# Down products of both FFNs in a seven-block form, with sums formed in the gates, in a hybrid decoder block

## The chip, the cores and the metric

The kernel runs on one core of one Trainium2 chip. The metric is the device time of one execution in microseconds (us). Below, TensorE is PE (its weight loads PEld), VectorE is DVE, ScalarE is ACT, GpSimd is POOL, and SyncE is SP, which here only issues DMAs.

## The reference, cut to what matters

One decoder block: a SwiGLU FFN, three mixers in parallel behind one projection, a second SwiGLU FFN, and a final norm. All data is float32; the sequence has 1024 tokens, the model width D is 1024 and the FFN width 2816 (22 tiles of 128).

```python
def _swiglu(h, w_gate, w_up, w_down):
    return (jax.nn.silu(h @ w_gate) * (h @ w_up)) @ w_down

x = x + 0.5 * _swiglu(_rmsnorm(x, ffn1_norm), ffn1_w_gate, ffn1_w_up, ffn1_w_down)
h = _rmsnorm(x, mix_norm)
...                                   # RWKV-7, NSA
y_mem = _memory_branch(q_mem, _rmsnorm(mem, mem_norm), mem_w_k, mem_w_v)   # 256 memory tokens
...                                   # gated merge, x = x + merged @ w_out
x = x + 0.5 * _swiglu(_rmsnorm(x, ffn2_norm), ffn2_w_gate, ffn2_w_up, ffn2_w_down)
return _rmsnorm(x, final_norm)
```

## The kernel before, in words

Everything is held transposed: x is eight strips of 128 features by 1024 tokens, and each strip has two halves of 512 tokens. To keep float32 accuracy on PE every operand is split into a high and a low part (`split`: ACT writes the high part, DVE, or POOL where it is asked to, subtracts it from the source for the low part), and each product of 128 x 128 weights with 128 x 512 data is three matmuls (`mm3`: high x high, high x low, low x high).

An FFN has two stages. The **gates** (class `Gates`) compute silu(gate) * up for the 22 tiles. The first four tiles are computed plainly; the other 18, in nine pairs, by `run`, which already uses a seven-block form: of a 2 x 2 block product it computes seven block products (P1 to P7, of four 128 x 512 products each) in place of eight, from sums and differences of weight blocks that POOL forms (`blocks`, tiles `wS` and `wraw`) and of data blocks that were formed once (`sums`). `finish` makes an activation tile `sg` out of a gate and an up product and SP stores it to HBM (`ad`). One pair of tiles takes two rounds of seven block products, one for gate and one for up; the last two blocks of a round (P4 and P3) are computed in the round behind it.

The **tail** (`Builder.tail`) is the down product. It loads the activations back (`wraw<-ad`), splits them into tiles `a`, loads and splits the down weights (`wd`), and for each strip d of the output and each half accumulates in a PSUM bank `pd` over the tiles of one chunk; DVE then adds a quarter of that to x. The 22 tiles are taken in chunks of 4, 5, 8 and 5. In the last chunk the strips of one half come before those of the other, so that sums of squares, the norm and its splits (`after`, in the background by `tick`) can start early. `xload` reloads x at the tail's start. In the first FFN the tail also normalizes the memory tokens on the side (`aside`, `Mem.tokens`), into tiles `mt` that the memory branch uses right after the tail.

Each engine runs its queue in order; the order in a queue comes out of a scheduler that places the instructions of the program as written. Weight blocks are fetched and split three products ahead (`AHEAD`). The raw weights have eight buffers in the FFN stages, their high and low parts four each. Temporary results of the gates go through a ring of ten buffers (`rg`).

## Time and profile before

| | |
|---|---|
| median of 3 runs | 2943.76 us (2938.05 to 2948.24) |
| profiled execution: its time | 2942.52 us |
| profiled execution: its span | 2940.7 us |
| PE busy | 2836.4 us, 96% of the span |
| DVE, ACT, POOL busy | 60%, 43%, 22% |
| first tail, from first to last `pd` matmul | 471.5 to 713.0 us |
| second tail | 2682.2 to 2923.9 us |

The profiled execution's own time is 1.8 us above its span. Busy shares are means over stages; which engine is waited for has to be read from each stage. A matmul's own duration overlaps that of the next, so the time that one costs is read from the number of matmuls in a stretch.

### The profile page before, as it was taken

Reading aid. Unit: us, or ns where it says so; the run is one execution under the profiler, and the core shown is the slowest. Engines: PE = TensorE matmul, PEld = TensorE weight load, DVE = VectorE, ACT = ScalarE, POOL = GpSimd, SP = SyncE. Lnnn points to the kernel's source line nnn. Section 1 sums busy time; section 2 is a strip of 40 time slices with the busy share of each in tenths; the row PEclk is TensorE's granted clock in tenths of the full one; section 3 lists DMA queues with packets and bytes.
Section 4 is the critical chain, followed back from the end, with each engine's and each line's share of the span. In section 5 each row is a group of like instructions: output and inputs, shape, how many; then the busy total and the mean of one; then the engine's idle time right before and its main releaser. Section 6 shows DMA issues by size and latency. Waiting matters only on the chain. (4 is left out here: it accounts for less than half of the span.)

```text
span 2940.7 us, 39952 instructions
## 1 busy us (share of the span) xinstructions
PE 2836.4 (96%) x13790; PEld 2252.7 (77%) x13790; DVE 1755.4 (60%) x3794; ACT 1276.1 (43%) x2743; POOL 638.0 (22%) x717
## 2 busy tenths in 40 slices
PE   7899999999999999999999989999998999999997
PEld 5788888887887777767767667778777888888886
DVE  8555555627566656766555357888857555555526
ACT  5333333315454445544443356666544333333313
POOL 3422220004011011111110133433323422220002
PEclk9999999999999999999999998999999999999999
DMA  4222226515313222222221552221475222225413
GB/s 154 76 85 84 86 78 203 162 36 150 96 61 91 60 66 71 65 73 63 65 65 59 158 169 77 84 60 58 145 224 177 90 86 79 83 83 193 141 41 106
DMA packets 203047, 294.41 MB, mean 100 GB/s; under 512 B 46131, under 2 KB 75707, under 8 KB 202844
## 3 DMA queue, kind: packets, MB, share of 16 engines
q1 hardware_dynamic: 186384, 263.25, 29.1%
q10 hardware_dynamic: 16460, 28.61, 3.3%
q8 instruction: 108, 1.77, 0.3%
q14 instruction: 95, 0.78, 0.1%
HBM read 223.51 MB, written 68.27 MB: 99 GB/s over the span
## 5 line engine op out<-in xcount | busy, mean ns | idle before, releaser
L99 ACT ACTIVATE whi<-wraw 128x512 fp32r<-128x512 f32 x576 | 345.3, 603 | 755.0 <-PE pgu L120 283.1
L102 DVE TENSOR_TENSOR wlo<-wraw,whi 128x512 fp32r<-128x512 f32 (+1 forms) x568 | 411.8, 729 | 375.2 <-ACT whi L99 349.5
L119 PE MATMUL mm<-h,whi 128*128 128x512 f32 x800 | 330.1, 413 | 0.2 <-ACT gbt L1553 0.2
L121 PE MATMUL mm<-h,wlo 128*128 128x512 f32 x800 | 320.6, 402 | 7.2 <-DVE wlo L102 7.2
L120 PE MATMUL mm<-h,whi 128*128 128x512 f32 x800 | 318.7, 398 | 0.0
L119 PE MATMUL pgu<-h,whi 128*128 128x512 f32 x688 | 272.5, 396 | 19.5 <-ACT whi L99 18.6
L121 PE MATMUL pgu<-h,wlo 128*128 128x512 f32 x688 | 271.9, 396 | 9.2 <-DVE wlo L102 9.1
L121 PE MATMUL pd<-a,wlo 128*128 128x512 f32 x704 | 274.2, 390 | 1.7 <-DVE wlo L102 1.7
L120 PE MATMUL pgu<-h,whi 128*128 128x512 f32 x688 | 272.0, 396 | 2.2 <-DVE h L94 1.7
L120 PE MATMUL pd<-a,whi 128*128 128x512 f32 x704 | 273.9, 389 | 0.0
L119 PE MATMUL pd<-a,whi 128*128 128x512 f32 x704 | 273.9, 389 | 0.0
L119 PE MATMUL pgu<-t,whi 128*128 128x512 f32 x576 | 224.3, 389 | 2.1 <-ACT rg L412 2.1
L120 PE MATMUL pgu<-t,whi 128*128 128x512 f32 x576 | 224.1, 389 | 0.0
L121 PE MATMUL pgu<-t,wlo 128*128 128x512 f32 x576 | 224.1, 389 | 0.0
L132 POOL TENSOR_TENSOR acc<-acc,sq 128x512 f32<-128x512 f32 x46 | 68.1, 1481 | 578.6 <-ACT sq L131 575.5
L121 PEld LDWEIGHTS mm<-h,wlo 128*128 128x128 f32 x800 | 151.6, 190 | 39.9 <-DVE wlo L102 9.0
L119 PEld LDWEIGHTS mm<-h,whi 128*128 128x128 f32 x800 | 151.8, 190 | 36.4 <-issue 5.3
L120 PEld LDWEIGHTS mm<-h,whi 128*128 128x128 f32 x800 | 151.9, 190 | 28.6 <-issue 3.0
L119 PEld LDWEIGHTS pgu<-h,whi 128*128 128x128 f32 x688 | 131.5, 191 | 49.4 <-ACT whi L99 21.6
L256 DVE SCALAR_TENSOR_TENSOR x<-pd,x 128x512 f32<-128x512 f32 x128 | 87.7, 688 | 130.2 <-PE pd L121 126.3
L121 PEld LDWEIGHTS pgu<-h,wlo 128*128 128x128 f32 x688 | 131.1, 191 | 40.3 <-DVE wlo L102 13.0
L121 PEld LDWEIGHTS pd<-a,wlo 128*128 128x128 f32 x704 | 132.2, 188 | 30.4 <-DVE wlo L102 3.0
(401 smaller groups left out, 6071.5 us busy)
## 6 DMA issues: line engine op xcount, KB each, us to landing
wraw<-in_wgu SPq DMA_DIRECT2D x192, 256.0 KB, 2.6
wraw<-in_wd SPq DMA_DIRECT2D x96, 256.0 KB, 2.7
ad<-sg SPq DMA_DIRECT2D x88, 256.0 KB, 2.8
wraw<-ad SPq DMA_DIRECT2D x88, 256.0 KB, 2.7
wraw<-in_win SPq DMA_DIRECT2D x52, 256.0 KB, 2.6
wraw<-in_wgb SPq DMA_DIRECT2D x48, 256.0 KB, 2.8
gd<-gbt SPq DMA_DIRECT2D x48, 256.0 KB, 2.0
gbt<-gd ACTq DMA_DIRECT2D x40, 256.0 KB, 2.7
```

The source lines that it names most:

```text
L99: nc.scalar.activation(hi, src, AF.Copy)
L102: (nc.vector if eng_lo == "dve" else nc.gpsimd).tensor_sub(lo, src, hi.bitcast(FT))
L119: mm(ps, w[0], x[0], start=start, stop=False, **kw)
L120: mm(ps, w[0], x[1], start=False, stop=False, **kw)
L121: mm(ps, w[1], x[0], start=False, stop=stop, **kw)
L132: eng.tensor_add(acc, acc, sq)
L256: nc.vector.scalar_tensor_tensor(x[d][:, c], p, 0.25, x[d][:, c], op0=OP.mult, op1=OP.add)
```

## The change

The down product of the tiles 4 to 21 takes the seven-block form too: output strips are taken in pairs (2dp, 2dp+1), tiles in pairs, tokens in halves. Seven block products over a chunk of three pairs of tiles (nine matmuls each) take the place of eight. The data blocks that this needs (the tile itself for three of the blocks, differences of the pair's four tiles for the other four) are formed in the gates by POOL, four subtractions for each pair, and stored: seven tiles for each pair where there were four. The weight sums of a chunk are formed in the tail by POOL, on 128 x 384 tiles. Of the seven products three go to x through ACT (a copy scaled by a quarter) and POOL (an addition), the other four as before through DVE. The first four tiles stay plain and come last. In the tail PSUM has seven banks where there were four; activations are kept in eight groups of three tiles, with four raw buffers (`ar`), and every second tile of three gets its low part from POOL. `sg` has seven buffers where it had five. The memory tokens are normalized in the first FFN's gates, stored to HBM (`td`), and fetched after the tail.

```diff
-CHUNKS = (("a", 4), ("p", 5), ("h", 8), ("p", 5))
+ORDER = "P1", "P2", "P6", "P5", "P7", "P3", "P4"
+NG = 8
+SG = 7
...
+        slots = [(self.hp, f"h{p}0{k}") for k in range(KT) for p in range(2)]
+        slots += [(ap, f"a{n}") for n in range(6 * NG - 32)]
+        slots += [(self.hp, f"h{p}1{k}") for k in range(KT) for p in range(2)]
+        bank = lambda: pool.tile([128, HALF], FT, name="pd", tag="dn", bufs=7)
+        temp = lambda tag, n, bufs: ap.tile([128, n], FT, name=tag, tag=tag, bufs=bufs)
+        groups = [ad[2 + 3 * c + j, name] for c in range(3) for name in ORDER for j in range(3)]
+        groups += [ad[f, half] for half in range(2) for f in range(4)]
+        def load(g):
+            for j, src in enumerate(groups[3 * g:3 * g + 3]):
...
+                if g < 3:
+                    raw = self.wraw(src, HALF)
+                else:
+                    raw = temp("ar", HALF, 4)
+                    nc.sync.dma_start(raw, src)
+                self.split(*t, raw, eng_lo="pool" if j == 1 else "dve")
+        def blocks(c, dp):
+            a = {(i, q): self.wraw(wd[2 * dp + i, :, (6 * c + 3 * q) * 128:(6 * c + 3 * q + 3) * 128], 384)
+                 for i, q in ((0, 0), (0, 1), (1, 0), (1, 1))}
+            yield self.wparts(a[0, 0])
+            yield self.wparts(a[0, 1])
+            s1, s2 = temp("ds", 384, 4), temp("ds", 384, 4)
+            nc.gpsimd.tensor_add(s1, a[1, 0], a[1, 1])
+            nc.gpsimd.tensor_sub(s2, s1, a[0, 0])
+            yield self.wparts(s2)
+            yield self.wparts(s1)
+            nc.gpsimd.tensor_sub(a[1, 0], a[0, 0], a[1, 0])
+            yield self.wparts(a[1, 0])
+            nc.gpsimd.tensor_sub(a[0, 1], a[0, 1], s2)
+            yield self.wparts(a[0, 1])
+            yield self.wparts(a[1, 1])
+        def copy_add(d, half, ps):
+            t = temp("dc", HALF, 4)
+            nc.scalar.activation(t, ps, AF.Copy, scale=0.25)
+            xd = x[d][:, halves[half]]
+            nc.gpsimd.tensor_add(xd, xd, t)
+        ops = [(c, dp, g, c * 7 + g) for c in range(3) for two in range(2) for g in range(7) for dp in (2 * two, 2 * two + 1)]
...
+        for g in range(3):
+            load(g)
+        for dp in range(2):
+            for d in (2 * dp, 2 * dp + 1):
+                xload(d)
+        for g in range(3, NG):
+            load(g)
+        for n, (c, dp, i, g) in enumerate(ops):
+            while len(got) < min(len(ops), n + 1 + AHEAD):
+                pull()
...
+            for k in range(3):
+                self.mm3(ps, [a[:, k * 128:k * 128 + 128] for a in w], act[3 * g + k], ...)
...                                       # P1, P6, P7: copy_add; P2, P5, P3, P4: add
+            if dp == 3 and 3 * (g + NG) < len(groups):
+                load(g + NG)
+        for half in range(2):
+            for d in range(KT):
+                w = self.wload(wd[d, :, 18 * 128:22 * 128], 512)
+                ps = bank()
+                for f in range(4):
+                    self.mm3(ps, [a[:, f * 128:f * 128 + 128] for a in w], act[63 + 4 * half + f], f == 0, f == 3)
+                add(d, half, ps)
+                self.tick()
+                after(half, d)
... Gates.finish
-        nc.sync.dma_start(self.ad[f][half], sg)
+        pair, n = f // 2, f % 2 * 2 + half
+        q = self.act.setdefault(pair, {})
+        q[n] = sg
+        if n != 1:
+            nc.sync.dma_start(self.ad[pair, ("P1", None, "P2", "P3")[n]], sg)
+        if len(q) == 4:
+            a11, a12, a21, a22 = [q[j] for j in range(4)]
+            t = {j: self.ring() for j in ("P5", "P7", "P6", "P4")}
+            nc.gpsimd.tensor_sub(t["P5"], a12, a11)
+            nc.gpsimd.tensor_sub(t["P7"], a22, a12)
+            nc.gpsimd.tensor_sub(t["P6"], a22, t["P5"])
+            nc.gpsimd.tensor_sub(t["P4"], a21, t["P6"])
+            for j in t:
+                nc.sync.dma_start(self.ad[pair, j], t[j])
... Gates.run
+            if i > 20 and i % 5 == 0:
+                next(aside, None)
... Mem.tokens
-                B.split(self.hi[k + e], self.lo[k + e], a)
+            t = [ring().bitcast(FR) for _ in range(2)]
+            B.split(*t, raw)
+            for p in range(2):
+                nc.sync.dma_start(self.td[p][k:k + 2].rearrange("e p n -> p e n"), ...)
+    def fetch(self, tp):
+        self.hi, self.lo = [[tp.tile([128, 256], FR, name=f"mt{p}{k}") for k in range(KT)] for p in range(2)]
+        for k in range(KT):
+            for p, t in enumerate((self.hi, self.lo)):
+                self.nc.sync.dma_start(t[k].bitcast(FT), self.td[p][k])
```

Three places in the queues show what this does to the order.

**SP where the first FFN's gates end and its tail begins, before.** `ad<-sg` stores an activation tile, `x<-in_xT` reloads a strip of x, `wraw<-ad` loads an activation tile, `wraw<-in_wd1` down weights.

```order
L106 DMA wraw_4086<-ad70_165 128x512 [waits DMAHW5_49,DMAHW4_49,DVE_49]
L324 DMA ad211_194<-sg_3663 128x512 [waits DVE_49]
L324 DMA ad210_193<-sg_3707 128x512 [waits DMAHW6_49,DVE_49]
L106 DMA wraw_4090<-ad71_166 128x512 [waits DMAHW7_49,DMAHW1_49,DVE_49]
L324 DMA ad201_192<-sg_3749 128x512 [waits DMAHW0_49,DVE_49]
L106 DMA wraw_4047<-in_wd1 128x512 [waits DVE_49]
L106 DMA wraw_4094<-in_wd1 128x512 [waits DMAHW2_49,DVE_49]
L1530 DMA x0_3843<-in_xT 128x1024 [waits DMAHW3_49,PE_49]
L1530 DMA x1_3844<-in_xT 128x1024 [waits DMAHW4_49]
```

The same place now (`rg_4025` to `rg_4028` are the four differences of the last pair, `ar<-ad2P5` and the two behind it the three tiles of the fourth group, P5):

```order
L381 DMA ad10P2_216<-sg_3900 128x512 [waits DMAHW4_49,DVE_49]
L390 DMA ad10P5_218<-rg_4025 128x512 [waits DMAHW5_49,Pool_49]
L390 DMA ad10P7_219<-rg_4026 128x512 [waits DMAHW6_49,Pool_49]
L390 DMA ad10P6_217<-rg_4027 128x512 [waits DMAHW7_49,Pool_49]
L390 DMA ad10P4_221<-rg_4028 128x512 [waits DMAHW0_49,Pool_49]
L1610 DMA x0_4044<-in_xT 128x1024 [waits DMAHW1_49,PE_49]
L1610 DMA x1_4045<-in_xT 128x1024 [waits DMAHW2_49]
L1610 DMA x2_4046<-in_xT 128x1024 [waits DMAHW3_49]
L1610 DMA x3_4047<-in_xT 128x1024 [waits DMAHW4_49]
L248 DMA ar_4118<-ad2P5_162 128x512 [waits DMAHW5_49,DVE_49]
L248 DMA ar_4124<-ad3P5_169 128x512 [waits DMAHW6_49]
L248 DMA ar_4130<-ad4P5_176 128x512 [waits DMAHW7_49]
```

The reloads of x and the loads of the fourth group now stand behind four stores that wait for POOL, where the x reloads stood behind a store that waits for DVE.

**POOL at the same place, before.** The last weight sums of the gates, then the first work of the tail's end (sums of squares, `acc`):

```order
L375 TENSOR_TENSOR wS_3686<-wS_3685,wraw_3599 128x512 [waits DMAHW1_49,DVE_49,Pool_49]
L378 TENSOR_TENSOR wraw_3603<-wraw_3599,wraw_3603 128x512
L381 TENSOR_TENSOR wraw_3601<-wraw_3601,wS_3686 128x512 [waits DMAHW3_49,DVE_49,Pool_49]
L132 TENSOR_TENSOR acc_4321<-acc_4321,sq_4383 128x512 [waits Activation_49]
L132 TENSOR_TENSOR acc_4321<-acc_4321,sq_4446 128x512 [waits Activation_49,Pool_49]
```

And now (the four differences of the last pair, the four weight sums of the first pair of strips, `ds` and `wraw`, additions to x, the low part of a P5 tile):

```order
L385 TENSOR_TENSOR rg_4025<-sg_3942,sg_3759 128x512 [waits DVE_49,Pool_49]
L386 TENSOR_TENSOR rg_4026<-sg_3856,sg_3942 128x512 [waits DMAHW4_49]
L387 TENSOR_TENSOR rg_4027<-sg_3856,rg_4025 128x512 [waits Pool_49]
L388 TENSOR_TENSOR rg_4028<-sg_3900,rg_4027 128x512 [waits Pool_49]
L259 TENSOR_TENSOR ds_4251<-wraw_4210,wraw_4212 128x384 [waits DMAHW7_49,DMAHW5_49,PE_49]
L260 TENSOR_TENSOR ds_4252<-ds_4251,wraw_4206 128x384 [waits DMAHW1_49,PE_49,Pool_49]
L263 TENSOR_TENSOR wraw_4210<-wraw_4206,wraw_4210 128x384
L265 TENSOR_TENSOR wraw_4208<-wraw_4208,ds_4252 128x384 [waits DMAHW0_49,DMAHW4_49,Activation_49,Pool_49]
L277 TENSOR_TENSOR x0_4044<-x0_4044,dc_4248 128x512 [waits DMAHW1_49,Activation_49]
L277 TENSOR_TENSOR x0_4044<-x0_4044,dc_4321 128x512 [waits Activation_49]
L277 TENSOR_TENSOR x2_4046<-x2_4046,dc_4269 128x512 [waits DMAHW3_49]
L104 TENSOR_TENSOR act311_4123<-ar_4124,act310_4122 128x512 [waits DMAHW6_49,DMAHW2_49,Activation_49]
```

POOL had nothing to do at the tail's start and now has a row of work in which additions wait for x to land and a split waits for a P5 tile. The four weight sums of the second pair of strips stand right behind the last row.

**POOL in the middle of the first gates, before:** the weight sums of two rounds.

```order
L374 TENSOR_TENSOR wS_3385<-wraw_3303,wraw_3305 128x512 [waits DMAHW3_49,DMAHW2_49]
L375 TENSOR_TENSOR wS_3386<-wS_3385,wraw_3299 128x512 [waits DMAHW5_49,DVE_49,Pool_49]
L378 TENSOR_TENSOR wraw_3303<-wraw_3299,wraw_3303 128x512
L374 TENSOR_TENSOR wS_3535<-wraw_3455,wraw_3457 128x512 [waits DMAHW7_49,DMAHW6_49,DVE_49]
L378 TENSOR_TENSOR wraw_3455<-wraw_3451,wraw_3455 128x512 [waits DMAHW1_49,DVE_49,Pool_49]
L381 TENSOR_TENSOR wraw_3301<-wraw_3301,wS_3386 128x512 [waits DVE_49]
```

And now:

```order
L441 TENSOR_TENSOR wS_3567<-wraw_3485,wraw_3487 128x512 [waits DMAHW5_49,DMAHW4_49]
L442 TENSOR_TENSOR wS_3568<-wS_3567,wraw_3481 128x512 [waits DMAHW7_49,DVE_49,Pool_49]
L445 TENSOR_TENSOR wraw_3485<-wraw_3481,wraw_3485 128x512
L385 TENSOR_TENSOR rg_3469<-sg_3320,sg_3137 128x512 [waits DVE_49]
L386 TENSOR_TENSOR rg_3470<-sg_3234,sg_3320 128x512 [waits DMAHW3_49]
L387 TENSOR_TENSOR rg_3471<-sg_3234,rg_3469 128x512 [waits Pool_49]
L388 TENSOR_TENSOR rg_3472<-sg_3278,rg_3471 128x512 [waits Pool_49]
L441 TENSOR_TENSOR wS_3717<-wraw_3637,wraw_3639 128x512 [waits DMAHW1_49,DMAHW0_49,Activation_49]
L445 TENSOR_TENSOR wraw_3637<-wraw_3633,wraw_3637 128x512 [waits DMAHW3_49,Activation_49,Pool_49]
L448 TENSOR_TENSOR wraw_3483<-wraw_3483,wS_3568 128x512 [waits DVE_49]
```

The four differences of the pair before stand between the third weight sum of one round and the first of the next; the fourth sum of the first round (`wraw_3483<-wraw_3483,wS_3568`) stands three rows behind them.

## Rows read from the trace of the kernel before

**Rows 1.** The page's first part: busy time, share of the span and instructions of each engine.

```profile
PE 2836.4 (96%) x13790; PEld 2252.7 (77%) x13790; DVE 1755.4 (60%) x3794; ACT 1276.1 (43%) x2743; POOL 638.0 (22%) x717
```

**Rows 2.** Busy time by stretches (start and end, length, then for each engine busy time and number of instructions, the granted clock, the DMA share, GB/s): three stretches of the first tail, and the second FFN's gates.

```profile
471.00:500.00 29.00, 29.00 (x130) 24.02 (x129) 17.53 (x28) 8.28 (x14) 0.00 (x0) 1.00 0.84 298
...
550.00:600.00 50.00, 50.00 (x222) 41.43 (x221) 28.29 (x54) 16.59 (x32) 0.00 (x0) 1.00 0.47 147
600.00:650.00 50.00, 50.00 (x223) 41.40 (x222) 12.29 (x19) 5.83 (x10) 0.00 (x0) 1.00 0.12 33
...
2440.00:2682.00 242.00, 240.97 (x1064) 199.27 (x1062) 129.17 (x185) 94.44 (x163) 60.40 (x45) 1.00 0.31 95
```

**Rows 3.** The instructions that touch `pd`, by stretches of the two tails (columns PE, PEld, DVE, clock, DMA share, GB/s).

```profile
471.00:715.00 244.00, 240.52 (x1056) 198.04 (x1056) 43.14 (x63) 1.00 0.42 131
2682.00:2930.00 248.00, 240.03 (x1056) 198.18 (x1056) 43.87 (x64) 0.99 0.36 112
```

**Rows 4.** Who waited for whom from 470 to 700 us (us in total, times, longest us); PE is in none of the rows.

```profile
ACT whi L99 <- PE pd L120: 89.3, 32, 7.8
...
ACT a L99 <- DMA wraw<-ad: 32.6, 14, 10.3
```

**Rows 5.** Groups of instructions by form (out<-in, count, then busy us and mean ns of one), from the answers for POOL and ACT over the whole span and for DVE from 471 us on.

```profile
L374 POOL TENSOR_TENSOR wS<-wraw 128x512 f32<-128x512 f32 x36 | 46.5, 1291 | 207.6 <-DMA wraw<-in_wgu 175.1 <-DVE wlo L102 32.5
...
L788 POOL TENSOR_TENSOR bk<-k,ecs 128x128 f32<-128x128 f32 x32 | 14.3, 447 | 17.0 <-PE sm L792 10.1 <-DVE k L724 6.8
...
L99 ACT ACTIVATE whi<-wraw 128x512 fp32r<-128x512 f32 x528 | 331.4, 630 | 740.0 <-PE pgu L120 283.1 <-PE pd L120 195.8 <-PE mm L120 106.9
...
L99 ACT ACTIVATE whi<-wraw 128x128 fp32r<-128x128 f32 x48 | 14.7, 307 | 15.0 <-PE pd L120 13.6
...
L102 DVE TENSOR_TENSOR a<-wraw,a 128x512 fp32r<-128x512 f32 x80 | 52.7, 689 | 27.9 <-ACT a L99 27.7
```

**Rows 6.** The timeline around 61 us, where DVE and POOL both have work (start us, duration us, instruction, count); `sg<-sg,pgu` reads PSUM, the other DVE rows read two SBUF tiles.

```profile
61.25 1.67 POOL L349 TENSOR_TENSOR x<-rg,x 128x512 f32<-128x512 f32 x1 [3.64 <-DVE h L102]
...
67.98 3.41 POOL L349 TENSOR_TENSOR x<-rg,x 128x512 f32<-128x512 f32 x2
71.35 3.38 POOL L350 TENSOR_TENSOR rg<-rg 128x512 f32<-128x512 f32 x2
...
59.89 0.68 DVE L102 TENSOR_TENSOR wlo<-wraw,whi 128x512 fp32r<-128x512 f32 x1
60.49 1.28 DVE L102 TENSOR_TENSOR h<-x,h 128x512 fp32r<-128x512 f32 x2
...
63.40 3.47 DVE L102 TENSOR_TENSOR h<-x,h 128x512 fp32r<-128x512 f32 x2
66.79 0.68 DVE L321 TENSOR_TENSOR sg<-sg,pgu 128x512 f32<-128x512 f32 x1
...
70.19 3.42 DVE L102 TENSOR_TENSOR h<-x,h 128x512 fp32r<-128x512 f32 x2
```

**Rows 7.** The timeline where the first gates end and the tail begins: PE's first `pd` matmul, DVE's last sum and product of the gates and its first addition to x, SP's issues (duration is that of all in the row), and ACT's first activation split that waited.

```profile
471.52 0.39 PE L119 MATMUL pd<-a,whi 128*128 128x512 f32 x1
...
471.72 0.69 DVE L416 TENSOR_TENSOR rg<-pgu,rg 128x512 f32<-128x512 f32 x1 [1.43 <-PE pgu L121]
472.44 0.69 DVE L321 TENSOR_TENSOR sg<-sg,rg 128x512 f32<-128x512 f32 x1
...
481.10 2.63 DVE L256 SCALAR_TENSOR_TENSOR x<-pd,x 128x512 f32<-128x512 f32 x4 [1.94 <-DMA x<-in_xT]
...
474.80 3.71 SPq L1530 DMA_DIRECT2D x<-in_xT  x6
478.92 0.92 SPq L106 DMA_DIRECT2D wraw<-ad  x2
...
488.09 1.27 ACT L99 ACTIVATE a<-wraw 128x512 fp32r<-128x512 f32 x2 [10.25 <-DMA wraw<-ad]
```

**Rows 8.** DMA issues (count, KB each, median us from issue to landing).

```profile
wraw<-ad SPq DMA_DIRECT2D x88, 256.0 KB, 2.7
...
x<-in_xT SPq DMA_DIRECT2D x8, 512.0 KB, 7.9
```

**Rows 9.** The first gates: a row of the waits from 100 to 470 us, and two of POOL's timeline (in brackets its idle time before, and what ended it).

```profile
ACT whi L99 <- PE pgu L120: 159.5, 90, 4.1
...
395.38 1.74 POOL L378 TENSOR_TENSOR wraw<-wraw 128x512 f32<-128x512 f32 x1
404.30 1.29 POOL L374 TENSOR_TENSOR wS<-wraw 128x512 f32<-128x512 f32 x1 [7.19 <-DMA wraw<-in_wgu]
```

**Rows 10.** Busy time by short stretches behind the first tail (columns as in rows 2).

```profile
718.00:720.00 2.00, 0.53 (x5) 0.33 (x3) 1.97 (x2) 1.10 (x3) 0.81 (x1) 1.00 0.76 208
720.00:723.00 3.00, 1.90 (x7) 1.33 (x8) 2.89 (x6) 2.51 (x7) 1.73 (x2) 0.88 0.49 130
723.00:726.00 3.00, 3.00 (x16) 2.90 (x16) 0.81 (x2) 0.96 (x3) 3.00 (x3) 0.55 0.49 114
```

**Rows 11.** PE's first matmuls behind the first tail: the memory branch's keys, and a wait of the projections among them.

```profile
712.81 0.28 PE L119 MATMUL S<-mt,whi 128*128 128x256 f32 x1
...
720.40 0.40 PE L962 MATMUL mm<-wvh,h 128*128 128x280 f32 x1 [1.87 <-ACT wvh L99]
```

More of the change, by code (lines that the diff above doesn't have):

```diff
@@ L224, in tail @@
         ap = st.enter_context(self.tc.tile_pool(name="ffa", bufs=1, reuse_waits="tile"))
-        ps = st.enter_context(self.tc.tile_pool(name="ffd", bufs=1, space=PSUM, reuse_waits="tile"))
-        def parts(kind, j):
-            if kind == "p":
-                return [[ap.tile([128, HALF], FR, name=f"a{p}{j}{half}") for p in range(2)] for half in range(2)]
-            a, b = divmod(j, 4)
-            return [[self.hp.tile([128, HALF], FR, name=f"a{p}{j}{half}", tag=f"h{p}{a}{2 * b + half}")
-                     for p in range(2)] for half in range(2)]
@@ L258, in tail @@
[L258 to L285 removed]
+        pool = st.enter_context(self.tc.tile_pool(name="ffd", bufs=1, space=PSUM, reuse_waits="tile"))
@@ L1473, in body @@
     nc.vector.tensor_copy(B.ones, one)
-    M = Mem(B, A, lambda m, j: yd[2][m][j // 2][:, (j % 2) * 256:(j % 2) * 256 + 256])
+    td = [drp.tile([KT, 128, 256], FT, name=f"td{p}") for p in range(2)]
+    M = Mem(B, A, lambda m, j: yd[2][m][j // 2][:, (j % 2) * 256:(j % 2) * 256 + 256], td)
     def ring_of(st):
@@ L1532, in body @@
                           lambda half, d: nc.sync.dma_start(x1d[d][:, halves[half]], x[d][:, halves[half]])),
[L1533 removed]
+                   st)
     with ExitStack() as mid:
@@ L1565, in body @@
         with ExitStack() as st:
+            mt = st.enter_context(tc.tile_pool(name="met", bufs=1, reuse_waits="tile"))
+            M.fetch(mt)
             M.open(st)
```

123 lines of the change are left out of this document (59 added, 64 removed).

## The prediction

> **What bounds the kernel now.** I read the page's busy shares first: PE is busy 96% of the span, the others 60% and less [rows 1]. Then the stretches, since only a stage tells what work taken from PE is worth there. In both tails PE is busy in every microsecond at full clock, one matmul for each 0.225 us (222 in 50 us), and ACT, DVE and POOL have room [rows 2, 3]. Then the waits of the first tail: ACT waits for PE to free weight buffers, 89.3 us in all, and for activation loads; PE waits for nobody [rows 4]. The gates look alike: 241 of 242 us busy [rows 2], ACT waiting for PE [rows 9]. So these stages end with PE, and a matmul less is worth its 0.225 us as long as what the change hands to POOL, DVE, ACT and the queues stays ahead of PE. The sum below is made against the profiled execution, 2942.5 us, which is 1.2 us under the median of 2943.8.
>
> **What it removes.** Of the tail's 1056 matmuls [rows 3], 18 tiles x 8 strips x 2 halves x 3 = 864 become seven eighths, 756: 108 fewer in each tail, 216 in all. At 0.225 us that is **-48.6 us**. Everything else gives some of it back.
>
> **The start of each tail: +13 us each.** Let 0 be the tail's first matmul (471.5 in the first tail). The last activation of the gates is done at +1.6 (472.44 + 0.69) [rows 7]. Now POOL forms four differences. One such subtraction takes 1.29 us alone [rows 5] and 1.70 where DVE works beside it (two in 3.41) [rows 6]; four take 5.2 to 6.8, and I take 6.2 since DVE has some splits there: +7.8. Until then SP's queue is blocked by the fourth store, and behind it stand four reloads of x and the three tiles of the fourth group (P5). Issues follow each other by 0.62 us (six in 3.71) [rows 7], so they go out from +8.4 to +12.1. They are 2.75 MB, and the queue moved 298 GB/s at this place before [rows 2], so 9.2 us: the P5 tiles have landed at about +17.6. The rows have the same pile-up: two activation loads issued at 478.92 behind 3 MB of x were waited for until 488.09, 9.2 us [rows 7]. It cost nothing then, as four tiles fed PE for 192 matmuls, 43 us; now three groups feed it for six products of nine matmuls, 12 us.
>
> PE meanwhile: four products to +8.1. The fifth (P6 of the first pair of strips) needs two weight sums that stand behind the differences on POOL. A 128x384 sum is no row; between 447 ns (128 columns) and 1291 (512) [rows 5] the line gives 1.01 us. So +9.8, with ACT's split (0.52, on the line from 307 to 630) +10.3: PE idles 2.2 us and ends this product at +12.4. P5 starts after a split of 0.63 [rows 5] at +18.2, 5.8 us idle. Then the second pair of strips: its sums stand on POOL behind additions that wait for x and behind the low part of the second P5 tile (ACT at +18.9, POOL +20.2); two sums make it +22.2, three ACT splits +23.8, and 18 matmuls, P5 and P6 mixed, end at +27.8. Eight products unhindered take 16.2: 11.6 us late. An idle PE also loses its clock: behind the first tail, after 1.5 us idle of 2, 0.88 and then 0.55 was granted in the next two stretches of 3 us, most of the second at the lower of its two levels, 1.2 GHz [rows 10]: 1.7 us lost; here a part falls into waiting, so 1.3. Bounds: 7.8, if the P5 tiles land 2.7 us after their issue like a median load [rows 8] (2.8 less), POOL runs undisturbed (1 less) and the clock stays; 16.9, if two more strips of x (1 MB, 3.4 us) get ahead of them and POOL is always disturbed.
>
> **The middle of each tail: +3 us each.** DVE and POOL disturb each other where DVE reads two SBUF tiles: at 61 to 75 us both backlogged, each does one instruction per 1.70 us, where DVE alone needs 0.60 (59.89 to 60.49), so one of POOL keeps DVE out for 1.10; a DVE row with a PSUM input in between took its usual 0.68 [rows 6]. On 384 columns I scale to 0.83 and 0.45. In the second half of a chunk (14 products, 28.4 us of PE) POOL has 8 weight sums, 6 additions and 7 splits, 20.9 us, DVE 14 weight and 14 activation splits, 14.7: 35.6 us that can't lie beside each other, 7.2 too many. The first half has 19.5. Only the first two chunks have such a full half; the third loads 8 tiles in place of 21. Weights are ready three products ahead, 6.1 us, and the POOL results of that half are needed later, so most is made up in the half behind: I take 1.5 us for each full half. Bounds: 0 and 7.2.
>
> **The smaller terms: +3.5 us together.** In the second half of the first tail's end DVE has per output tile a weight split, an addition, a normalization and its split, 4 x 0.60 = 2.4, and POOL's sum of squares, 1.10, against 12 matmuls, 2.7: 0 to 0.8 for 8 tiles, 1.5 in all. Before, 15 matmuls (3.4) covered it. The fetch of the memory tokens: half of its 16 loads stand on SP behind the last store of x, so they land up to 8 x 0.62 + 2.7 = 7.7 us after the tail. The keys followed the tail at once [rows 11], but projections of the first half can go between, and waits of 1.9 us stood there already: 1, bounds 0 and 5. The gates: POOL's chain ends at most 1.6 + 6.8 = 8.4 us after a pair's last product; the first sum behind it that PE needs is three POOL instructions on, about +13, and its product starts six products of 12 matmuls later, at +16.2. POOL idled for stretches of 7 us [rows 9]. The extra stores and the memory tokens' instructions also lie beside PE. I take 1 for all this. Edits at nothing: `sg` buffers, the weights' new order in HBM, three PSUM banks more; they add no instruction, and work that PE is busy with covers any wait of theirs.
>
> Sum: 2942.5 - 48.6 + 26 + 6 + 3.5 = 2929.4, **2929 us**.
>
> **Rivals.** *The loads are hidden after all (2908 us).* The start then costs only the 2.2 us before the fifth product, 10.8 less in each tail. For it: SP's queue is shared, but 16 engines may serve small loads before the strips of x. Against it: the activation loads of before, which waited as long as the bytes ahead of them.
>
> *DVE and POOL decide the middle (2952 us, slower).* If the 7.2 us of a full half reach PE wholly, a tail loses 14.4 in place of 3: +22.8. It decides from the point where DVE's low parts of the weights are more than three products (6.1 us) late. For it: DVE's queue has activation splits between the weight splits, and when POOL has a backlog each DVE split pays 1.10 first. Against it: most POOL results are needed half a chunk later, and the first half of a chunk has 8.9 us to spare. The Trainium skill's page "SBUF — State Buffer", section "SBUF: two separate sides", states this rule: the port pair that DVE and GpSimd share is an exclusive lock held for a whole instruction, also against a DVE instruction with two SBUF inputs. By that rule with nothing made up the time would be this 2952; the trace agrees with the lock (1.70 against 0.60), and how much of it reaches PE no row shows.
>
> *The chains in the gates reach PE (2976 us, slower).* If half of 5.2 us of differences stood before a needed sum in each of 18 pairs, that is 47 us. It decides where the needed sum is later than +16.2. For it: POOL waits on loads, which an SP queue with three more stores per pair delays. Against it: 3 us of margin by the order, and 60 of 242 us that POOL is busy [rows 2].
>
> **How the numbers follow.** Forecast 0.50, with a range of its own of 2918 to 2942; hidden loads 0.20; DVE and POOL 0.20; gates 0.10. A measurement here can tell about 0.3%, 8.8 us. Below 2935 lie 0.37 of the forecast and all of the hidden loads: faster 0.57. Within lie 0.13 of the forecast, 0.08 of the DVE and POOL case and 0.02 of the gates: same 0.23. Slower 0.20. The range, 2904 to 2953, leaves out the best third of the hidden loads (0.06), the worse third of DVE and POOL (0.06) and most of the gates (0.08).
>
> **What would show it.** 948 `pd` matmuls in each tail. In the first 30 us of each tail two idle stretches of PE, about 2 and 6 us, the longer ended by ACT's split of an activation tile that waited for its DMA, and x reloads issued about 8 us after the first `pd` matmul. DVE splits above 1 us in the second half of the first two chunks. No new wait of PE in the gates. I am wrong if the x reloads go out earlier, if PE waits for low parts of weights all through the chunks, or if the gates become longer.

## The result, and the profile after

The changed kernel takes 2958.1 us (median of 10 runs, 2954.1 to 2965.4) against 2941.9 us of the kernel before beside it (2938.1 to 2950.0): 1.0055 of its time, 95% interval 1.0042 to 1.0069. It is slower, where 2929 us and a gain were forecast. The profiled execution took 2956.2 us with a span of 2954.4, 13.7 above the span before.

The busy times of the page of the changed kernel, beside [rows 1]:

```profile
PE 2804.6 (95%) x13574; PEld 2212.6 (75%) x13574; DVE 1943.0 (66%) x3852; ACT 1369.7 (46%) x2923; POOL 1041.9 (35%) x1005
```

PE has its 216 matmuls fewer and is 32 us less busy, yet the span grew: PE now waits, which it did not do in the tails before. Where, the first tail by stretches shows (the view of [rows 2]: start and end, length, then busy time and instructions of PE, PEld, DVE, ACT and POOL, granted clock, DMA share, GB/s):

```profile
485.00:500.00 15.00, 8.57 (x20) 5.67 (x20) 9.42 (x10) 5.69 (x11) 10.39 (x9) 0.59 0.72 260
...
530.00:560.00 30.00, 24.70 (x101) 17.75 (x99) 28.51 (x30) 16.52 (x32) 24.65 (x18) 1.00 0.63 192
...
590.00:620.00 30.00, 29.08 (x129) 23.57 (x127) 29.98 (x31) 18.40 (x36) 22.84 (x16) 1.00 0.61 186
...
650.00:680.00 30.00, 30.00 (x134) 24.82 (x134) 20.07 (x26) 13.19 (x25) 11.31 (x8) 1.00 0.37 104
```

An undisturbed stretch of 30 us holds 134 matmuls (last row). From 485 to 500 us only 20 run, in place of 67, at a granted clock of 0.59; from 530 to 560, where DVE is busy 28.5 of 30 us and POOL 24.7, 101 run. From 590 to 620 DVE and POOL are about as busy, and 129 run.

For comparing kernels I use two stretches of the first tail and count `pd` matmuls: the first 58 us from its first matmul ("start") and the next 120 ("middle"; nothing is lost later). The columns are PE and PEld, DVE, ACT where it has rows, clock, DMA share, GB/s. The kernel before, then the changed one:

```profile
471.50:529.50 58.00, 57.98 (x256) 48.05 (x256) 13.20 (x20) 1.00 0.65 217
529.50:649.50 120.00, 119.69 (x529) 98.89 (x529) 18.33 (x27) 1.00 0.32 95
```

```profile
472.50:530.50 58.00, 46.69 (x176) 35.77 (x177) 5.45 (x8) 4.66 (x8) 0.85 0.63 213
530.50:650.50 120.00, 111.45 (x474) 87.32 (x473) 21.85 (x32) 13.34 (x23) 1.00 0.49 147
```

The start is 80 matmuls short, 18.0 us at 0.225 us each, and the middle 55, 12.4 us. The forecast had 13 and 3. These counts differ from run to run: in e1_spread, e8_fetch_act and e15_after_banks (the three repeats, below), whose queues have the changed kernel's order in the tail, the start is 72, 67 and 70 short and the middle 62, 53 and 57. The rest of the change is small: the first tail begins 1.0 us later (472.5, before 471.5), the part between the tails is 1.0 us longer, the part behind the second 2.1.

**The start.** PE's long waits, what SP, POOL, ACT and DVE did (start us, duration, in brackets the idle time before and what ended it):

```profile
474.65 1.29 POOL L385 TENSOR_TENSOR rg<-sg 128x512 f32<-128x512 f32 x1 [14.04 <-DVE sg L371]
...
475.97 4.18 SPq L390 DMA_DIRECT2D ad10P<-rg  x4
480.24 1.82 SPq L1610 DMA_DIRECT2D x<-in_xT  x4
482.16 0.39 SPq L248 DMA_DIRECT2D ar<-ad2P  x1
...
482.13 0.63 ACT L101 ACTIVATE act<-wraw 128x512 fp32r<-128x512 f32 x1 [9.09 <-DMA ad10P<-rg]
...
483.71 0.80 PE L121 MATMUL pd<-act,whi 128*128 128x512 f32 x1 [2.85 <-ACT whi L101]
490.47 0.80 PE L121 MATMUL pd<-act,whi 128*128 128x512 f32 x1 [1.20 <-ACT act L101]
494.30 0.79 PE L122 MATMUL pd<-act,whi 128*128 128x512 f32 x1 [3.03 <-DVE act L104]
501.23 0.80 PE L123 MATMUL pd<-act,wlo 128*128 128x512 f32 x1 [2.50 <-DVE wlo L104]
...
492.51 0.69 DVE L271 SCALAR_TENSOR_TENSOR x<-pd,x 128x512 f32<-128x512 f32 x1 [5.58 <-POOL x L277]
```

The chain is the one forecast: POOL's differences, SP's four stores, then the reloads of x (7.7 us behind the first matmul, forecast 8.4) and P5's loads; the fifth product begins at +11.2 us (forecast 10.3) and P5 at +17.9 (18.2). Two things were not in it. ACT's split of the ninth activation tile waited for the fourth store, since the tile lies in the memory that this store reads. And the low parts of P5 stood in DVE's queue behind an addition that waited for POOL's addition to the same strip. Nor was the clock's share as small as I took it. PE's granted clock in stretches of 2 us (PE, clock, DMA share, GB/s):

```profile
482.00:484.00 2.00, 0.29 (x1) 0.93 0.91 330
484.00:486.00 2.00, 1.02 (x3) 0.50 1.03 416
486.00:488.00 2.00, 2.00 (x5) 0.50 1.02 405
488.00:490.00 2.00, 1.27 (x3) 0.50 1.05 403
490.00:492.00 2.00, 0.80 (x1) 0.50 0.82 327
492.00:494.00 2.00, 0.00 (x0) 0.50 0.00 0
494.00:496.00 2.00, 1.70 (x4) 0.50 0.24 48
496.00:498.00 2.00, 2.00 (x7) 0.65 0.80 282
498.00:500.00 2.00, 0.72 (x4) 1.00 0.97 274
500.00:502.00 2.00, 0.77 (x2) 0.70 0.67 199
502.00:504.00 2.00, 2.00 (x7) 0.50 0.44 125
```

After 2.85 us without work it stood at 0.50, the lower of its two levels (1.2 GHz), from 484 to 496, although PE worked for all of 486 to 488, and again from 502 to 504, behind the idle 2.5 us before 501.2. By the spacing of the `pd` matmuls in these 58 us, 23 of them came 0.3 to 0.6 us after the one before, most of these 0.43, which I count as 5.0 us lost to the clock, and six gaps above 0.7 us lost 13.1; in the second tail 24 and five, 4.7 and 11.2.

**The middle.** Who waited for whom, PE in the 120 us of the middle (us in total, times, longest), and POOL and DVE between 543 and 549 us:

```profile
PE pd L123 <- DVE wlo L104: 7.9, 11, 2.1
PE pd L121 <- ACT whi L101: 0.5, 1, 0.5
```

```profile
543.31 0.54 DVE L104 TENSOR_TENSOR wlo<-wraw,whi 128x384 fp32r<-128x384 f32 x1
...
547.63 1.36 DVE L104 TENSOR_TENSOR wlo<-wraw,whi 128x384 fp32r<-128x384 f32 x1
...
544.58 1.01 POOL L259 TENSOR_TENSOR ds<-wraw 128x384 f32<-128x384 f32 x1 [2.34 <-DVE act L104]
...
547.12 1.45 POOL L260 TENSOR_TENSOR ds<-ds,wraw 128x384 f32<-128x384 f32 x1
```

At 543.31 POOL has nothing to do and DVE's low part takes 0.54 us; at 547.63 POOL works and the same instruction takes 1.36. In the first tail as a whole (groups by form: count, busy us, mean ns):

```profile
L104 DVE TENSOR_TENSOR act<-ar,act 128x512 fp32r<-128x512 f32 x41 | 53.6, 1311 | 3.0 <-ACT act L101 2.9
L104 DVE TENSOR_TENSOR wlo<-wraw,whi 128x384 fp32r<-128x384 f32 x57 | 53.2, 940 | 9.0 <-ACT whi L101 9.0
L271 DVE SCALAR_TENSOR_TENSOR x<-pd,x 128x512 f32<-128x512 f32 x62 | 42.5, 685 | 31.0 <-PE pd L123 21.7 <-POOL x L277 9.1
L104 DVE TENSOR_TENSOR wlo<-ds,whi 128x384 fp32r<-128x384 f32 x24 | 27.3, 1145 | 3.4 <-ACT whi L101 3.4
```

An activation split took 0.69 us before [rows 5] and takes 1.31. PE waits for low parts of weights.

Where in the chunks it waits, the starts of the `pd` matmuls show. A half of a chunk is 14 products, 126 matmuls, which took 28.6 us in the kernel before. What each half took beyond that:

| half | first tail, us | second tail, us |
|---|---|---|
| first of chunk 1 (the start) | 17.9 | 15.3 |
| second of chunk 1, full | 6.2 | 6.4 |
| first of chunk 2 | 3.5 | 4.2 |
| second of chunk 2, full | 0.0 | 0.2 |
| first of chunk 3 | 3.5 | 3.5 |
| second of chunk 3 | 0.0 | 0.0 |

PE's waits in the first halves of chunks 2 and 3 (553.8 to 585.8 and 614.4 to 646.4 us), the same row twice, and one of DVE's rows in the second of these:

```profile
PE pd L123 <- DVE wlo L104: 2.2, 4, 0.9
```

```profile
623.53 1.16 DVE L104 TENSOR_TENSOR act<-ar,act 128x512 fp32r<-128x512 f32 x1 [0.26 <-ACT act L101]
```

So only the first of the two full halves loses time itself. The second loses nothing, but DVE still makes its activation splits 9 us into the half behind it (623.5, that half begins at 614.4), and PE meets late low parts in the first five products there. Behind the first full half it is the same.

### The profile page after: what moved, and what is told of

It reads as the page before. It is cut to its first block, busy times and chain, and to the rows that moved or that the text cites. A ratio compares the mean times of both kernels' runs of the same rounds, so it can differ in the third digit from the quotient of the medians.

```text
span 2954.4 us, 40599 instructions
## 1 busy us (share of the span) xinstructions
PE 2804.6 (95%) x13574; PEld 2212.6 (75%) x13574; DVE 1943.0 (66%) x3852; ACT 1369.7 (46%) x2923; POOL 1041.9 (35%) x1005
## 5 line engine op out<-in xcount | busy, mean ns | idle before, releaser
L104 DVE TENSOR_TENSOR wlo<-wraw,whi 128x512 fp32r<-128x512 f32 (+1 forms) x576 | 463.0, 807 | 294.8 <-ACT whi L101 281.0
L101 ACT ACTIVATE whi<-wraw 128x512 fp32r<-128x512 f32 (+1 forms) x584 | 352.9, 607 | 650.1 <-PE pgu L122 252.7
L123 PE MATMUL pd<-act,wlo 128*128 128x512 f32 x632 | 253.6, 402 | 23.5 <-DVE wlo L104 23.1
L121 PE MATMUL pd<-act,whi 128*128 128x512 f32 x632 | 250.2, 396 | 10.5 <-ACT whi L101 6.8
L122 PE MATMUL pd<-act,whi 128*128 128x512 f32 x632 | 249.6, 395 | 5.2 <-DVE act L104 5.2
L122 PEld LDWEIGHTS mm<-h,whi 128*128 128x128 f32 x800 | 151.4, 189 | 28.5 <-issue 3.0
L123 PEld LDWEIGHTS pd<-act,wlo 128*128 128x128 f32 x632 | 121.0, 191 | 63.8 <-DVE wlo L104 38.8
L121 PEld LDWEIGHTS pgu<-h,whi 128*128 128x128 f32 x688 | 131.6, 191 | 49.2 <-ACT whi L101 21.6
L122 PEld LDWEIGHTS pgu<-h,whi 128*128 128x128 f32 x688 | 131.1, 191 | 31.9 <-DVE h L96 2.7
L121 PEld LDWEIGHTS pd<-act,whi 128*128 128x128 f32 x632 | 120.6, 191 | 37.5 <-ACT whi L101 9.4
```

Of the source, the lines that this page charges most:

```text
L101: nc.scalar.activation(hi, src, AF.Copy)
L104: (nc.vector if eng_lo == "dve" else nc.gpsimd).tensor_sub(lo, src, hi.bitcast(FT))
L121: mm(ps, w[0], x[0], start=start, stop=False, **kw)
L122: mm(ps, w[0], x[1], start=False, stop=False, **kw)
L123: mm(ps, w[1], x[0], start=False, stop=stop, **kw)
```

## The experiments

"Short" is the count of `pd` matmuls under 256 in the start and under 529 in the middle of the first tail.

| run | time, us | of the kernel before, 95% interval | short: start, middle |
|---|---|---|---|
| changed kernel | 2958.1 | 1.0055 (1.0042 to 1.0069) | 80, 55 |
| e1_spread | 2958.0 | 1.0052 (1.0030 to 1.0075) | 72, 62 |
| e2_act_stores | 2961.2 | 1.0070 (1.0045 to 1.0095) | 81, 57 |
| e3_no_sums | 2936.0 | 0.9986 (0.9974 to 0.9998) | 81, 2 |
| e4_add_dve | 2940.6 | 0.9998 (0.9985 to 1.0010) | 58, 28 |
| e5_tokens_only | 2954.7 | 1.0040 (1.0021 to 1.0059) | 0, -2 |
| e6_diff_dve | 2951.6 | 1.0034 (1.0021 to 1.0048) | 60, 46 |
| e7_start | 2973.5 | 1.0111 (1.0087 to 1.0134) | 80, 58 |
| e8_fetch_act | 2958.8 | 1.0060 (1.0043 to 1.0077) | 67, 53 |
| **e9_adds_diff** | **2930.2** | **0.9962 (0.9949 to 0.9975)** | 55, 22 |
| e10_adds_diff_p5 | 2934.0 | 0.9977 (0.9967 to 0.9986) | 60, 16 |
| e11_adds_diff_met | 2932.1 | 0.9967 (0.9955 to 0.9979) | 47, 26 |
| e12_all | 2928.9 | 0.9968 (0.9951 to 0.9984) | 58, 12 |
| e13_banks | 2931.8 | 0.9965 (0.9952 to 0.9978) | 53, 25 |
| e14_banks_met | 2933.0 | 0.9965 (0.9953 to 0.9978) | 43, 32 |
| e15_after_banks | 2960.2 | 1.0049 (1.0033 to 1.0066) | 70, 57 |

### The middle: POOL's work taken away, or moved

e3_no_sums, which leaves out the sums of down weights (cut):

```
-  nc.gpsimd.tensor_add(s1, a[1, 0], a[1, 1])     # and the three
-  nc.gpsimd.tensor_sub(s2, s1, a[0, 0])          # others like it
-  yield self.wparts(s2); yield self.wparts(s1)
+  yield self.wparts(a[1, 0]); yield self.wparts(a[1, 1])
```

> The changed kernel without the four sums and differences of down weights on POOL: the products P6, P5, P7 and P3 take plain blocks of the weights, so the output is not the reference's. DVE, ACT and PE have the same instructions as before, POOL 24 per half chunk pair fewer (8 in each half of a chunk). Theory (POOL keeps DVE out, and only therefore are the low parts late): splits of 384 columns on DVE fall from a mean of 0.81 us to about 0.65, the later loss of each tail falls from 14 or 15 us to 3 to 6, the start loses 2 to 3 us less because no sum stands behind the differences, and the time is 2928 to 2938. Rival (DVE has too much work of its own in these halves): the later loss stays above 10 us and the time is 2945 to 2957.

Its middle, columns as above:

```profile
529.30:649.30 120.00, 119.91 (x527) 98.50 (x526) 22.50 (x33) 15.09 (x26) 1.00 0.48 144
```

The middle holds 527 matmuls with all of DVE's instructions in place: its loss is gone, and 22 us of the time. (By halves from the second on it loses 1.9, 0.0, 0.0 and 0.8 us.) The start, 81 short, did not gain. This alone does not part POOL's hold on DVE from the time that PE waits for a sum as such. In e4_add_dve the sums stay, DVE gets more work, POOL less.

```
-  copy_add(2 * dp, 0, ps)         # P1; P6 and P7 likewise
+  add(2 * dp, 0, ps)
```

> The changed kernel with the 36 additions of a tail that ACT copies and POOL adds to x (P1, P6, P7) made by DVE straight from PSUM, as for the other products. POOL has 6 instructions of 128x512 fewer in each half chunk, DVE 6 of 0.68 us more, ACT 6 fewer; the weight sums stay. Theory (POOL's two-input instructions keep DVE out, and an addition from PSUM does not mind): a full half has some 28 us that exclude each other in place of 35.6, and the loss behind the first half chunk falls from 14 or 15 us to 4 to 8; time 2938 to 2948. Rival (DVE has too much of its own work): 4 us more of it in every half chunk, the loss grows to 18 us or more; time 2962 to 2975.

Its start and middle, and its groups of DVE's splits in the first tail:

```profile
470.80:528.80 58.00, 50.14 (x198) 38.87 (x197) 12.38 (x19) 0.91 0.67 232
528.80:648.80 120.00, 116.69 (x501) 92.78 (x500) 40.18 (x59) 1.00 0.48 143
```

```profile
L104 DVE TENSOR_TENSOR wlo<-wraw,whi 128x384 fp32r<-128x384 f32 x57 | 42.1, 741 | 1.4 <-ACT whi L101 1.4
L104 DVE TENSOR_TENSOR act<-ar,act 128x512 fp32r<-128x512 f32 x41 | 40.3, 991 | 5.6 <-ACT act L101 5.4
L104 DVE TENSOR_TENSOR wlo<-ds,whi 128x384 fp32r<-128x384 f32 x24 | 18.3, 764 | 0.9 <-ACT whi L101 0.9
```

DVE makes 36 additions more in each tail, and its splits become shorter all the same (1311 to 991 ns, 940 to 741, 1145 to 764). The loss of the middle halves, from 55 to 28 matmuls. (By halves from the second on: 2.9, 3.9, 0.0 and 0.6 us, so the half behind the first full one gains nothing.) That excludes the rival that DVE has too much work of its own: with less on POOL, DVE's splits are shorter although DVE does more. One thing it does not part. In the changed kernel DVE's additions waited 9.1 us for POOL's additions to the same strip, 5.6 of it in the start and 3.5 in the middle, and e4_add_dve has no such waits; how much of the gain is theirs is not shown. The start is 22 matmuls better than in the changed kernel and 9 better than in the best of the three repeats. That would fit additions waiting for x no longer standing in POOL's queue; it was not tried by itself.

e1_spread was to load the activations more evenly:

```
-  if dp == 3 and 3 * (g + NG) < len(groups):
-      load(g + NG)
+  if n in due and 3 * due[n] < len(groups):   # 24 products, not 14
+      load(due[n])
```

> The changed kernel with one thing different: the 21 activation tiles of the next chunk are loaded and split over 24 products, ten groups' distances of 3 or 4 products, in place of one group behind every second of the 14 products of the second half. In the changed kernel's profile a tail loses 18 and 15.5 us up to the second half of its first chunk and another 14 to 15 us from there to its last section. Theory (DVE and POOL are overbooked in the halves that load, and PE pays): with the loads spread neither half is overbooked, the later loss falls from 14 or 15 to 3 to 6 us in each tail, the first one stays, and the time falls by about 20 us to 2936 to 2942. Rival (the low parts are late because of their place in DVE's queue or because of the work behind them, not because of how much there is): the loss stays and the time is 2953 to 2961.

The order in the queues of SP, ACT, DVE and POOL came out the same row for row as in the changed kernel: it is not set by where the loads stand in the code. So the edit tried nothing, and the run is a repeat: tails of 245.9 and 245.7 us, against 246.3 and 245.7, but between them 1981.9 us, against 1970.6. The same program differs by 11 us there from one execution to the next. Whether spread loads would help was not tried.

### The start

e6_diff_dve:

```
+  eng = nc.vector if pair == 10 else nc.gpsimd
-  nc.gpsimd.tensor_sub(t["P5"], a12, a11)     # and the other three
+  eng.tensor_sub(t["P5"], a12, a11)
```

> The changed kernel with the four differences of the last pair of each FFN made by DVE (0.69 us each) and not by POOL (1.29 each); the order of every queue is otherwise the same. Theory (the start waits on the chain differences, stores, landing of the fourth store, split of the ninth activation tile that lies in the memory that the store reads, weight sums, the split of P5 behind them): the differences end 2.5 us earlier, the weight sums 5 us, PE's first idle stretch falls from 3 us to under 1, P6 of the first strips starts at 8 to 9.5 us and P5 at 15 to 16 in place of 17 to 18; the start loses 12 to 14 us in place of 15.5 to 18, time 2950 to 2954. Rival (transfers set the start): P5 starts at 17 to 18 as before and the time is 2954 to 2961.

Its start, and from its timeline the first matmuls of the fifth product and of P5:

```profile
472.70:530.70 58.00, 49.77 (x196) 37.54 (x197) 6.84 (x10) 5.24 (x9) 0.94 0.69 234
```

```profile
481.25 0.50 PE L121 MATMUL pd<-act,whi 128*128 128x512 f32 x1 [0.19 <-ACT whi L101]
487.54 0.74 PE L121 MATMUL pd<-act,whi 128*128 128x512 f32 x1 [3.81 <-ACT act L101]
```

The stretch ahead of the fifth product falls from 2.85 to 0.19 us, P5 begins at +14.8 us (487.5 - 472.7), 3.1 earlier, as the chain theory had it (8 to 9.5 and 15 to 16 us, here +8.5 and +14.8). The start holds 20 matmuls more than the changed kernel's, and 7 to 12 more than the three repeats. The time is 6.5 us less, within the theory's 2950 to 2954, though the two intervals against the kernel before just overlap.

e2_act_stores let ACT issue the last pair's four difference stores (`(nc.scalar if pair == 10 else nc.sync).dma_start(...)`):

> The changed kernel with one thing different: the four difference stores of the last pair are issued by ACT and not by SP, so the reloads of x stand behind no store that waits for POOL (the fourth reload still waits for POOL by its memory). Theory (the start loses its 15 to 18 us because the loads of P5 and x are issued 8 to 10 us into the tail): three reloads of x go out at the tail's first products, the P5 tiles land 3 to 5 us earlier, and the start loses 10 to 13 us; the time falls by 8 to 14 us to 2944 to 2950. Rival (the transfers themselves take this long, or POOL's queue is what is late): the start keeps its 15 to 18 us and the time is 2953 to 2961.

Nothing was won (81 short). The loads of P5 were issued 7.7 us behind the first matmul in place of 9.6, but ACT's own chain got longer: its split of the ninth tile now came at 483.4, 11.9 us behind the first matmul (9.6 in the changed kernel), the fifth product at +13.5 and ACT reached P5's tiles only behind the copy of that product, at 489.9. The stores left one queue and held up another.

e7_start took the differences on DVE, gave the ninth tile other memory (the tiles in `hp` ahead of those in `ap`), and put P5's loads ahead of two reloads of x:

> The changed kernel with three edits at the start of the tail: the differences of the last pair on DVE; the ninth activation tile and those behind it lie in the memory of the gates' own activations and no longer in that of the difference ring, so its split waits for no store; the loads of P5 are issued behind two reloads of x in place of four. Theory (as for the run with the differences alone): no idle stretch over 1.5 us before P6, P5's tiles landed by 13 us, the start loses 4 to 8 us in place of 15.5 to 18 and the later loss stays at 14 to 15; time 2934 to 2942. Rival (the bytes at this place take their time in whatever order, 3 MB with the weights at 300 to 400 GB/s): the start keeps 12 us or more; time 2949 to 2957.

It is 15 us slower than the changed kernel, where 16 to 24 us less were expected. Up to the fifth product PE waits for nothing (+8.2) and P5 begins at +14.5, but the start ends 80 matmuls short all the same. What came next was as late as what it had replaced; from its timeline, SP's issue of the next weights and the wait that PE had for them:

```profile
509.56 5.97 SPq L108 DMA_DIRECT2D wraw<-in_wd  x8
...
516.30 0.50 PE L121 MATMUL pd<-act,whi 128*128 128x512 f32 x1 [3.38 <-ACT whi L101]
```

The weights of the next strips were issued 38.3 us behind the first matmul, in e6_diff_dve 33.9, because SP's queue stood at loads of activations that waited for one of four `ar` buffers. Where the rest of the 15 us went was not settled; 11 us of it show behind the first tail (the 300th matmul there at 67.3 us, 56.2 in the changed kernel), where the new places of the tiles may hold the normalized strips up.

### The memory tokens

e5_tokens_only is the kernel before with this part of the change alone (tokens normalized in `run`'s `aside`, `fetch` behind the tail):

> The kernel before with the second part of the change alone: memory tokens normalized in the gates and fetched after the first tail, the tail in its old form. Theory (this part costs nothing that can be measured): 2939 to 2945 us, no more than 1 us in the gates and 2 behind the first tail. Rival (the 16 loads behind the tail, or the normalizing in the gates, hold PE): 2947 to 2952.

It costs 0.40% by itself, some 12 us, more than even the rival had; the price that I took, 1 us for the fetch and a part of 1 for the gates, was wrong. Its first key matmul in the timeline, and the stretch around it (columns as in the first table of stretches):

```profile
718.71 0.76 PE L119 MATMUL S<-mt,whi 128*128 128x256 f32 x2 [3.99 <-DMA mt<-td]
```

```profile
717.00:720.00 3.00, 1.19 (x4) 0.93 (x4) 3.00 (x4) 1.95 (x4) 2.86 (x3) 0.50 0.49 166
```

PE waits 4.0 us for the fetch (and then 2.0 for the norm), falls to the lower clock, and the 300th matmul behind the tail is 9.6 us later than before (62.3, before 52.7); its first tail begins 1.3 us later. In the changed kernel it is 3.5 later (56.2), though its keys wait longer, and for something else (its timeline):

```profile
726.88 0.55 PE L121 MATMUL S<-mt,whi 128*128 128x256 f32 x1 [7.70 <-DVE x L271]
```

That is an addition to x of the last output tiles, which has to free a PSUM bank: the seven banks. (In e1_spread, the same program, the same 7.7 us are put down to the fetch, so the row alone does not decide.) I tried the fetch on ACT's queue (e8_fetch_act, `nc.scalar.dma_start`), four banks of their own for the last section (e15_after_banks: a second pool of 4 behind the chunks), and, on e9_adds_diff, the fetch moved into the first tail (e11_adds_diff_met, with seven groups of activations to make room), the banks (e13_banks), and both (e14_banks_met):

> The changed kernel with the 16 loads of the memory tokens behind the first tail issued by ACT and not by SP, where they stand behind the last stores of x. Theory (those stores hold up the loads, the keys start 8 us behind the tail in place of 0.2, and 2 to 4 us of it are left after 1000 matmuls): the keys start within 4 us of the tail's end and the middle part is 1 to 4 us shorter, which the time, 2953 to 2958, shows barely. Rival (the keys wait for the landing or for something else): they start 6 us or more behind the tail and the time is 2955 to 2961.

> The changed kernel with four PSUM banks of its own for the last section of each tail, nothing else. Theory: keys start 4 to 5 us behind the tail (the fetch), the end of the second tail is unchanged or 1 us shorter; time 2953 to 2958. Rival (the fetch alone): keys 8 us late, time 2955 to 2961.

> The run with both edits, with seven in place of eight groups of activation tiles, and in the room that this gives the memory tokens fetched while the first tail's second chunk half runs, in place of behind the tail. Theory (the fetch behind the stores of x delays the keys): the keys start within 1 us of the tail's end, and the middle part is 2 to 4 us shorter at its 1000th matmul; seven groups cost nothing, as a group is wanted 15 products after its buffer comes free; time 1 to 4 us under the run with both edits. Rival (the loads come later with seven groups and the chunks wait for activations): 3 us or more above it.

> The run with additions and last differences on DVE, and the last section of a tail takes its sums in four PSUM banks of its own (as the tail before did) and not in seven. Theory (the keys wait for the bank of one of the last seven output tiles, whose addition DVE makes late): keys start within 5 us of the tail's end, where the fetch of the tokens then holds them; time 0 to 3 us under the run without. Rival (the fetch alone holds them): they start 8 us late as before.

> The same with the memory tokens fetched inside the first tail. Theory (banks and fetch each hold the keys 4 to 8 us, so only both edits help): keys start within 1 us of the tail's end, the middle part is 3 to 6 us shorter at its 1000th matmul than in the run with both DVE edits; time 2924 to 2929. Rival (something else holds them): 6 us or more, time as without.

The keys begin behind the first tail: changed kernel 8.1 us, ACT's fetch 6.3, banks 5.0, fetch in the tail 10.9, banks on e9_adds_diff 5.0, both 4.2. So the banks did hold them, but something else now stands in their place. The fetch inside the tail, which was to bring the keys within 1 us, did not; PE's waits in e13_banks from 704 to 716 us:

```profile
PE S L121 <- ACT h L101: 4.6, 1, 4.6
PE S L122 <- DMA mt<-td: 1.0, 1, 1.0
```

That is ACT's queue, and then the fetch. At the 1200th matmul behind the tail these runs are 2.3 to 5.4 us later than before, e9_adds_diff 4.0, and no time differs by more than its interval. This border costs some 2 to 5 us in these kernels; which wait would have to go last stays open.

### Together

> The changed kernel with the two edits that helped alone: all additions to x on DVE from PSUM (that run was 17 us under the changed kernel) and the last pair's differences on DVE (6.5 us under it). Theory (two separate losses, POOL's work in the chunks and POOL's chain at the start): the gains add, but the first already shortened the start by 3 to 5 us, so 2934 to 2939, with 6 to 9 us lost up to the second half of the first chunk and 7 to 8 behind it. Rival (both act on the same wait): no more than the better of the two, 2939 to 2944.

Its start and middle:

```profile
471.10:529.10 58.00, 51.39 (x201) 38.86 (x201) 12.91 (x19) 0.94 0.71 238
529.10:649.10 120.00, 117.54 (x507) 94.00 (x506) 40.37 (x59) 1.00 0.46 142
```

The two edits add: 2930.2 us, 28 under the changed kernel and 0.38% under the kernel before, more than forecast for it. The start still lacks 55 matmuls, 12.4 us.

e10_adds_diff_p5 (`load(3)` ahead of the first reloads of x) and e12_all (this and the fetch in the tail):

> The run with both edits, and the loads of P5 put ahead of two of the four first reloads of x in the program. Theory (P5's tiles wait for the bytes of x ahead of them): P5 starts 2 to 3 us earlier, the start loses 3 to 6 us, time 2930 to 2936. Rival (the additions, which now stand in DVE's queue ahead of P5's splits, wait for x all the same, as in the run with three edits at the start, which lost more later than it won): same time as the run with both edits, or 2 to 5 us more.

> All of these edits: additions and last differences on DVE, P5's loads ahead of two reloads of x, memory tokens fetched inside the first tail with seven groups. Theory: 2927 to 2935, under the kernel before by 0.2 to 0.5%. Rival (the earlier P5 costs later what it wins): 2936 to 2942, no difference from the kernel before.

P5's loads first win nothing: P5 began earlier, then one product of the second strips stood 6.1 us for weights whose sums came late, and the start is 60 short, not 55. e12_all, 2928.9 us, can't be told from e9_adds_diff.

## Why the prediction was wrong, point by point

**What bounds the kernel, and what is removed: right.** 948 `pd` matmuls in each tail, 216 fewer in all; the tails have no other idle time than the one that the change brings.

**The middle: the step that failed.** The forecast worked out 35.6 us of work in a full half that DVE and POOL can't do beside each other, against 28.4 us of PE, 7.2 too many. Then it said that "most is made up in the half behind" and took 1.5 for each full half, 3 us for each tail. That discount is the term that was mis-sized. The middle of the first tail lost 12.4 us, 9.4 more than forecast, in both tails some 19 of the 27 us between 2929 and the profiled 2956. By halves, the two tails lost 13.2 and 14.3 us behind the first half of chunk 1, where two full halves with nothing made up are 14.4. The half behind did not make it up: it lost 3.5 to 4.2 us itself, though the forecast gave it 8.9 us to spare, with DVE's leftover splits still in its queue among the low parts that PE needed there. That the sum comes so near to 14.4 is partly luck: the first full half with the half behind it lost 9.7 us, the second 3.5, and why they differ is not shown. The rival "DVE and POOL decide the middle (2952)" had the mechanism, and had 0.20.

The rule that stood beside that rival, from the Trainium skill's page "SBUF — State Buffer", section "SBUF: two separate sides", says that the port pair which a DVE instruction with two SBUF inputs shares with GpSimd goes to one instruction at a time and that the other fully blocks. The trace agrees: 0.54 us alone, 1.36 beside POOL, and shorter splits where POOL has less to do, though DVE has more. The 2952 us that go with nothing made up lie near the measured 2958, but that is luck in part: the excess came back in the sum and not in each half, and the start lost more than the 13 us in that figure.

**The start: chain right in the main, one term too small, two waits missed.** 18.0 us in the first tail and 15.9 in the second for 13 (bounds 7.8 to 16.9); the waits for the fourth store and for POOL's addition, told above, were not in it. The gaps lost 13.1 and 11.2 in the two tails, the forecast 11.6; the clock lost 5.0 and 4.7, for which I had taken 1.3 from one short stretch [rows 10]. Here the waits follow each other, and the lower level held from 484 to 496. That the first wait went in e6_diff_dve, and P5 came 3.1 us earlier, shows the chain; that e2_act_stores and e7_start took nothing off the loss shows that it is not one chain: what stands next in ACT's, DVE's and SP's queues is nearly as late.

**The small terms: sum right, terms wrong.** 3.5 us were forecast, and gates, middle part and end of this execution sum to 4.1. But moving the memory tokens costs some 12 us by itself in e5_tokens_only, and the "three PSUM banks more", costed at nothing, hold the keys 3 us longer (8.1 against 5.0 with four), though no time got shorter with four. That the middle part of the profiled execution was only 1.0 us longer was luck, since the same program took 11 us more there in e1_spread; this may also be why the medians differ by 16 us and the profiled executions by 14.

**The gates: right.** No new wait of PE there. The tail began 1.0 us later, which says little: in the three repeats, with the same gates, it began at 470.0, 470.9 and 473.3.

**Signs named in advance.** Right: 948 matmuls, reloads of x 8 us behind the first matmul, DVE splits above 1 us, nothing new in the gates. Half right: the two idle places in the start. They were 2.9 us for 2, and 1.2 and 3.0 together for 6. But the longer one ended with DVE's low part, which stood behind POOL, and not with ACT's split, and one of 2.5 us behind it was not named. What I had named as the sign of being wrong, PE waiting for low parts of weights all through the chunks, is what the waits show for the second half of the first chunk and for the halves behind the full ones: 7.9 of 8.4 us in the middle.

## What to carry to other kernels

Where two engines exclude each other, add up their work for each stretch in which the consumer may not wait. Here 13 to 14 of the 14.4 us in excess were lost. A later stretch with room on paper did not pay for it: the work left over stood there in the same queue as what the consumer needed next. A stage that was PE's can be lost to its helpers by an edit that takes a tenth of PE's work away and hands them the sums for it. And an addition whose source is in PSUM was better on DVE here, where POOL was the neighbour that hurt: it cost DVE 36 instructions a tail and made its splits 21 to 33% shorter.

## What the runs showed of the hardware that I had not expected

- The granted clock stayed at 0.50 for 12 us (484 to 496) with PE busy in 6.8 of them, while gaps of 1 to 3 us came one behind the other; behind the single gap of [rows 10] I had read 1.7 us.
- One and the same order of instructions took 1970.6 and 1981.9 us between the tails in two executions, while the tails agreed within 0.4 us. A change of 5 us there can't be read from one profile.
